# A decoder layer's first projection with GpSimd taken out: VectorE takes all modulation products, ScalarE takes h, TensorE takes the norm sum

## The chip, the cores and the metric

One NeuronCore of one Trainium2 chip runs the whole program. The time is device microseconds (us) of one execution. The engines are TensorE (PE in the profile, its weight loads PEld), VectorE (DVE), ScalarE (ACT), GpSimd (POOL) and SyncE (SP), which issues the DMAs. Each engine runs its own list of instructions in order; semaphores order them among each other.

## The reference

One decoder layer on 256 positions of 1024 channels. What matters here is its beginning:

```
mod = silu(c) @ w_ada + b_ada            # 6 x 1024 values: shift, scale, gate, twice
h   = rms_norm(x, norm1_g) * (1 + scale1) + shift1
proj = h @ w_in                          # q, k, v, z, xbc, dt
... attention on q, k, v; a state-space mixer on xbc, dt, z; output projection;
x = x + gate1 * mixed
x = x + gate2 * conv_ffn(rms_norm(x, norm2_g) * (1 + scale2) + shift2)
```

All arrays are float32.

## The kernel before

Activations lie transposed: channels on the 128 partitions, 256 positions along the free axis, so x is 8 tiles `xT[:, kt]`, and kt names a slice of 128 input channels. The first stage computes 16 blocks of 128 output channels (xbc, three blocks of z, and dt) in the 16 halves of the 8 PSUM banks, over the 8 slices, slice by slice, and in slice 0 also the part of v that comes from that slice.

For precision a product h·w is made from three float32r matmuls: whi·hhi, wlo·hhi and whi·hlo (`mm3`, L335). So each weight chunk is split after it lands: ScalarE rounds it into `whi` (L189) and VectorE subtracts to get `wlo` (L191). A slice has two chunks, of 1024 and of 912 columns. `P['subs']` says in how many pieces a chunk is loaded and split. A chunk in `PLAIN` is not split, but used as float32 in a single matmul, which PE runs in two passes. Here PE needs 8 x 16 = 128 products, that is 384 matmuls of 256 columns, for the 16 blocks.

h of a slice needs two sums over the 1024 inputs of c, the scale and the shift of those 128 channels (`mod`). Chunk 2·kt of `ada` gives the scale, chunk 2·kt+1 the shift. A chunk is multiplied with silu(c) (`cb`) and summed, either in one VectorE instruction (`ada_dve`, L239), or as a product on GpSimd (`ada_mul`, L244) that ScalarE then sums (`ada_sum`, L248). In the first stage chunks 0 and 1 and the odd ones go to VectorE, the 7 even ones from 2 on to GpSimd and ScalarE. `s1_next` lets GpSimd make `xr` = x times the norm's factor `rb` (L392). `s1_h` then makes the column `gcol` (L366), adds a bias (L253), and makes `hhi` on ScalarE (L380), `h` on VectorE (L384) and `hlo` on VectorE (L386).

The norm's factor for all positions comes first: squares `sq8`, added up into four tiles by VectorE, GpSimd and ScalarE, are summed over partitions by PE against ones (L267, in `rms_sum`), ScalarE takes the root (L270), VectorE the reciprocal (L272), and PE transposes it into PSUM (L291). PE runs 12 matmuls on ones ahead of that (L228) and 1 and 7 around the transposes (`keep_warm`, L296).

In this stage the order on every engine is the order of the code (`tc.manual_schedule`). SP issues its loads in the order of a list (`items`); a load of a weight chunk waits until the chunk 8 places earlier is split, and a load of `ada` until the chunk 9 places earlier is used. After the stage (from L450) the z projection (L785) and everything else follow, ordered by a scheduler within tables of units; the change leaves that code alone.

Of the kernel before, what the change touches and what calls it, by code (L numbers as in the profile page):

```python
# [11 lines left out]
AF = mybir.ActivationFunctionType  # L12
# [33 lines left out]

@with_exitstack
def mixer_ffn(ctx: ExitStack, tc: tile.TileContext, xT_d, c_d, vec_d, alog_d, ada_d,
# [272 lines left out]
    pool.memset(tri, 1.0)  # L321
    for o in (0, 256):
# [38 lines left out]
    first = list(range(12)) + [13, 12, 14, 15]  # L361
    final = (list(range(8)) + [12, 14, 15, 13, 8, 9, 10, 11], list(range(6)) + [14, 15, 12, 13, 8, 9, 10, 11, 6, 7],
             list(range(8)) + [14, 15, 12, 13, 8, 9, 10, 11], list(range(4)) + [14, 15, 12, 13, 8, 9, 10, 11, 4, 5, 6, 7])[P['final']]
    def s1_h(kt):
        g, shift = gcol[:, kt:kt + 1], mod[:, 2 * kt + 1:2 * kt + 2]
        dve.scalar_tensor_tensor(g, mod[:, 2 * kt:2 * kt + 1], sc1[:, kt:kt + 1], vec[:, V_N1 + kt:V_N1 + kt + 1],  # L366
                                 op0=OP.add, op1=OP.mult)
        ada_bias(2 * kt + 1, 2 * kt + 2)
        if kt == 0:
            xr = hbuf()  # L370
            if P["xr0"]:
                act.activation(rb, bank[7][:, 256:512], AF.Copy)
                pool.tensor_tensor(xr, xT[:, kt], rb, op=OP.mult)
            else:
                dve.tensor_tensor(xr, xT[:, kt], bank[7][:, 256:512], op=OP.mult)
        else:
            xr = X["xr"]
# [18 lines left out]
    def v0_mm(w):  # L396
        for j in range(2):
            c = slice(j * 512, j * 512 + 512)
            for t in range(2):
                o = bank[4 + 2 * j + t]  # L400
                pe.matmul(o, hhi[:, 0, blk(t)], w[0][:, c], start=True, stop=False)
                pe.matmul(o, hhi[:, 0, blk(t)], w[1][:, c], start=False, stop=False)
                pe.matmul(o, hlo[:, 0, blk(t)], w[0][:, c], start=False, stop=True)
        for j in range(2):
            c = slice(j * 512, j * 512 + 512)
            for t in range(2):
                o = bank[4 + 2 * j + t]
                if P["ev"][2 * j + t]:
                    dve.tensor_copy(vS[:, t, c], o)  # L409
                else:  # L410
                    act.activation(vS[:, t, c], o, AF.Copy)
# [8 lines left out]
    if P["scp"]:  # L420
        dve.tensor_scalar(sc1[:, 0:KT], vec[:, V_BADA:V_BADA + 16:2], 1.0, None, op0=OP.add)
    ada_dve(1)
    if not P["scp"]:
        dve.tensor_scalar(sc1[:, 0:KT], vec[:, V_BADA:V_BADA + 16:2], 1.0, None, op0=OP.add)
    for kt in range(KT):
        s1_h(kt)
        if kt < KT - 1:
            ada_mul(2 * kt + 2)
        if kt == 0:
            ws = [get(0)]  # L430
            w0 = get(0)
            ws.append(get(0))
        else:
            ws = [get(0), get(0)]
        if kt == 2:
            act.activation(warm, epsc, AF.Silu)
            dve.tensor_scalar(sc1[:, KT:], vec[:, V_BADA + 24:V_BADA + 32], 1.0, None, op0=OP.add)
            dve.scalar_tensor_tensor(gqk, vec[:, V_QG:V_QG + 1], SCALE, vec[:, V_KG:V_KG + 1], op0=OP.mult, op1=OP.mult)
        if kt < KT - 1:
            s1_next(kt + 1)  # L440
        if kt == 0:
            s1_mm(0, ws, first[:8])
            v0_mm(w0)
            s1_mm(0, ws, first[8:])
        else:
            s1_mm(kt, ws, final)
# [588 lines left out]
```

## Time and profile before

| | |
|---|---|
| median of 3 runs | 452.51 us (451.82 to 453.27) |
| profiled execution | 452.11 us, of which the span of instructions is 450.4 us |
| PE busy over the span | 433.8 us (96%) |
| DVE / ACT / POOL busy | 344.4 / 259.3 / 62.3 us |
| mean granted TensorE clock | 0.984 |

The span is from the first to the last instruction; what lies outside it is 1.7 us. The stage that the change touches takes the time up to the first z matmul (L785). Matmuls overlap, so PE's rows are longer than the distance from one to the next, and the distance is what one costs. The granted clock is 1.00 at 2.4 GHz and 0.50 at 1.2 GHz. The chip moved about 400 GB/s in the second to the fourth fortieth of the span, that is from 11 to 45 us.

### The profile page before, as it was taken

How to read it: one execution, taken by the hardware profiler on the slowest of the kernel's cores; microseconds unless marked ns; L12 is line 12 of the kernel's file. 1: busy time of each engine (PE TensorE's matmuls, PEld its weight loads, DVE VectorE, ACT ScalarE, POOL GpSimd, SP SyncE). 2: the span in 40 equal slices, each digit the busy share in tenths (PEclk: the TensorE clock that was granted, in tenths of full speed). 3: DMA queues.
4: the chain of work that ended last, by engine and by line, in shares of the span. 5: the costliest groups of instructions: out<-in, count | busy, mean ns of one | idle time of the engine just before them, and what ended most of it. 6: DMA issues, size and time to landing. Idle time of an engine off the chain costs nothing.

```text
span 450.4 us, 7730 instructions
## 1 busy us (share of the span) xinstructions
PE 433.8 (96%) x2900; PEld 384.7 (85%) x2900; DVE 344.4 (76%) x666; ACT 259.3 (58%) x523; POOL 62.3 (14%) x46
## 2 busy tenths in 40 slices
PE   7977999999999999999999989999999999999996
PEld 7876999867665566788899879999999999999996
DVE  4999992999567998647889478877777887777764
ACT  4535582945497668543237448566666665555540
POOL 3576400000000020100220000023322300000000
PEclk9789899999999999999999999999999999999999
DMA  7999674777558654245695073878677755654002
GB/s 287 399 402 400 203 239 149 255 283 268 175 175 283 229 207 182 94 141 188 222 412 206 20 307 110 282 246 258 228 254 260 234 185 186 193 174 156 0 1 95
DMA packets 31029, 96.71 MB, mean 215 GB/s; under 512 B 3712, under 2 KB 6672, under 8 KB 30992
## 3 DMA queue, kind: packets, MB, share of 16 engines
q1 hardware_dynamic: 30960, 96.20, 61.0%
q8 instruction: 23, 0.38, 0.4%
q14 instruction: 14, 0.11, 0.1%
q10 hardware_dynamic: 32, 0.02, 0.0%
HBM read 95.14 MB, written 1.06 MB: 214 GB/s over the span
## 4 chain that ended last, share of the span: by engine, by line
PE 73%; DMA 13%; DVE 7%; ACT 4%; SPq 1%; issue 1%; POOL 1%; DVEq 0%
PE bank L336 17%; PE bank L338 17%; PE bank L337 17%; PE bank L834 6%; DMA ada<-in_ada_dram 5%; PE bank L806 5%; PE bank L785 4%; DMA adax<-in_ada_dram 2%; DMA raw<-in_wv_dram 2%; DMA raw<-in_win_dram 2%; PE bank L906 1%; DVE wlo L191 1%; DMA xT<-in_xT_dram 1%; DVE ada L239 1%; DMA raw<-in_winq_dram 1%; DMA ab<-acd 1%
## 5 line engine op out<-in xcount | busy, mean ns | idle before, releaser
L191 DVE TENSOR_TENSOR wlo<-raw,whi 128x1024 fp32r<-128x1024 f32 (+3 forms) x112 | 137.4, 1235 | 15.4 <-ACT whi L189 15.0
L189 ACT ACTIVATE whi<-raw 128x1024 fp32r<-128x1024 f32 (+3 forms) x111 | 104.3, 953 | 36.7 <-PE bank L338 21.7
L336 PE MATMUL bank<-h2hi,whi 128*128 128x256 f32 x336 | 95.4, 285 | 2.1 <-ACT h2hi L876 1.9
L337 PE MATMUL bank<-h2hi,wlo 128*128 128x256 f32 x336 | 94.5, 283 | 0.0
L338 PE MATMUL bank<-h2lo,whi 128*128 128x256 f32 x336 | 93.9, 284 | 0.0
L336 PEld LDWEIGHTS bank<-h2hi,whi 128*128 128x128 f32 x336 | 64.4, 192 | 3.7 <-ACT h2hi L876 3.2
L244 POOL TENSOR_TENSOR ada<-ada,cb 128x1024 f32<-128x1024 f32 x13 | 33.4, 2569 | 241.8 <-DMA ada<-in_ada_dram 241.8
L337 PEld LDWEIGHTS bank<-h2hi,wlo 128*128 128x128 f32 x336 | 64.4, 192 | 0.0
L892 DVE SCALAR_TENSOR_TENSOR fbuf<-bank,vec,fbuf 128x255 f32<-128x255 f32 x84 | 40.4, 482 | 30.9 <-ACT fbuf L890 29.6
L338 PEld LDWEIGHTS bank<-h2lo,whi 128*128 128x128 f32 x336 | 63.8, 192 | 0.2 <-DVE h2lo L877 0.2
L336 PE MATMUL bank<-fsp,whi 128*128 128x256 f32 x176 | 49.8, 284 | 0.0
L337 PE MATMUL bank<-fsp,wlo 128*128 128x256 f32 x176 | 49.7, 283 | 0.0
L338 PE MATMUL bank<-fsp,whi 128*128 128x256 f32 x176 | 49.6, 283 | 0.0
L890 ACT ACTIVATE fbuf<-bank,vec 128x256 f32<-128x256 f32 x42 | 23.5, 561 | 36.4 <-PE bank L338 36.4
L806 PE MATMUL bank<-raw,h 128*128 128x512 f32 x96 | 44.3, 595 | 0.0
L336 PE MATMUL bank<-hhi,whi 128*128 128x256 f32 (+1 forms) x128 | 37.9, 296 | 3.7 <-DVE vS L409 2.4
L337 PE MATMUL bank<-hhi,wlo 128*128 128x256 f32 (+1 forms) x128 | 38.0, 297 | 2.2 <-DVE wlo L191 2.2
L338 PE MATMUL bank<-hlo,whi 128*128 128x256 f32 (+1 forms) x128 | 37.8, 295 | 0.7 <-DVE hlo L386 0.7
L336 PEld LDWEIGHTS bank<-fsp,whi 128*128 128x128 f32 x176 | 33.8, 192 | 0.1
L337 PEld LDWEIGHTS bank<-fsp,wlo 128*128 128x128 f32 x176 | 33.8, 192 | 0.0
L338 PEld LDWEIGHTS bank<-fsp,whi 128*128 128x128 f32 x176 | 33.7, 192 | 0.0
L239 DVE SCALAR_TENSOR_TENSOR ada<-ada,cb 128x1024 f32<-128x1024 f32 x25 | 30.3, 1216 | 3.5 <-DMA ada<-in_ada_dram 3.5
(222 smaller groups left out, 828.2 us busy)
## 6 DMA issues: line engine op xcount, KB each, us to landing
raw<-in_wup_dram SPq DMA_DIRECT2D x44, 512.0 KB, 4.2
ada<-in_ada_dram SPq DMA_DIRECT2D x38, 512.0 KB, 5.0
raw<-in_wdn_dram SPq DMA_DIRECT2D x22, 512.0 KB, 3.5
raw<-in_winq_dram SPq DMA_DIRECT2D x16, 512.0 KB, 4.3
raw<-in_wout_dram SPq DMA_DIRECT2D x16, 512.0 KB, 3.8
adax<-in_ada_dram SPq DMA_DIRECT2D x10, 512.0 KB, 7.6
raw<-in_win_dram SPq DMA_DIRECT2D x18, 256.0 KB, 7.0
raw<-in_winv_dram SPq DMA_DIRECT2D x6, 512.0 KB, 6.0
```

The lines of the kernel that those rows point to most:

```text
L189: act.activation(hi[:, c], t[:, c], AF.Copy)
L191: (pool if lo_on_pool(i) else dve).tensor_tensor(lo[:, c], t[:, c], hi[:, c].bitcast(F32), op=OP.subtract)
L239: dve.scalar_tensor_tensor(t, t, 1.0, sc, op0=OP.mult, op1=OP.mult, accum_out=mod[:, i:i + 1])
L244: pool.tensor_tensor(adas[i], adas[i], sc, op=OP.mult)
L336: pe.matmul(out, w[0], h[0], start=start, stop=False, skip_group_check=True)
L337: pe.matmul(out, w[1], h[0], start=False, stop=False, skip_group_check=True)
L338: pe.matmul(out, w[0], h[1], start=False, stop=stop, skip_group_check=True)
L785: pe.matmul(zo[i], w[:, blk(kt)], h32[:, kt, 0:S], start=(kt == 0), stop=(kt == KT - 1), skip_group_check=True)
L806: pe.matmul(bs[t], h32[:, kt, blk(t)], w[:, wc], start=(q4 == k2 == 0), stop=(kt == KT - 1))
L834: pe.matmul(sacc(d), w[:, blk(kt)], X["y32"][:, kt], start=(kt == d % 2 == 0), stop=(kt == 7), skip_group_check=True)
L890: act.activation(a, src, AF.Identity, bias=vec[:, V_FB + i:V_FB + i + 1], scale=vec[:, w + 2:w + 3])
L892: dve.scalar_tensor_tensor(a[:, s:], src[:, :S - s], vec[:, w + 2 - s:w + 3 - s], a[:, s:], op0=OP.mult, op1=OP.add)
```

## The change

- All 16 modulation products of the stage are `ada_dve` on VectorE; `ada_mul` and `ada_sum` are no longer called in it. `xr` is made by VectorE too. GpSimd has nothing to do in the stage after its masks.
- `h` is made by ScalarE from the same inputs as `hhi`.
- The 8 squares are 4 on ScalarE and 4 on VectorE, and PE sums all 8 (16 matmuls of one column in place of 8); GpSimd's square and VectorE's 4 adds are gone.
- 22 matmuls on ones in place of 12 ahead of the sums; 4 in place of 7 behind the transposes (`P['w1']`).
- The three terms run one after the other over the 8 blocks of a chunk: first whi·hhi for all, then wlo·hhi, then whi·hlo, except in the last slice, which keeps the old order. The second chunk of a slice is split behind the first chunk's matmuls in the code, and the next slice's products come behind that split.
- The v part of slice 0 (chunk 1, `-16` in `PLAIN`) is 4 float32 matmuls on `h` in place of 12 float32r ones, with no split. Its four copies out of PSUM are interleaved with the products.
- `P['subs']` is 1 for all slice chunks but the first: 10 chunks that were loaded and split in two pieces are now loaded and split in one. Chunk 1 (v) keeps its two loads.

```diff
-    for j in range(12):
+    for j in range(22):
         pe.matmul(bank[2][:, 0:128], ones, ones, start=True, stop=True)
...
-    pool.tensor_tensor(sq8[:, 3], xT[:, 3], xT[:, 3], op=OP.mult)
-    for kt in (5, 6, 7):
-        act.activation(sq8[:, kt], xT[:, kt], AF.Square)
-    for kt in (0, 1, 2, 4):
-        dve.tensor_tensor(sq8[:, kt], xT[:, kt], xT[:, kt], op=OP.mult)
-        if kt:
-            dve.tensor_tensor(sq8[:, 0], sq8[:, 0], sq8[:, kt], op=OP.add)
-    dve.tensor_tensor(sq8[:, 0], sq8[:, 0], sq8[:, 3], op=OP.add)
+    for kt in range(4, KT):
+        act.activation(sq8[:, kt], xT[:, kt], AF.Square)
+    for kt in range(4):
+        dve.tensor_tensor(sq8[:, kt], xT[:, kt], xT[:, kt], op=OP.mult)
+    def modulate1():
+        ada_dve(0)
+        dve.tensor_scalar(sc1[:, 0:KT], vec[:, V_BADA:V_BADA + 16:2], 1.0, None, op0=OP.add)
+        ada_dve(1)
+    r1 = rms_sum([sq8[:, kt] for kt in range(KT)], D, bank[7], modulate1)
...
+    def s1_gain(kt):
+        if kt:
+            ada_dve(2 * kt)
+            X["xr"] = hbuf()
+            dve.tensor_tensor(X["xr"], xT[:, kt], rb, op=OP.mult)
+            ada_dve(2 * kt + 1)
+        dve.scalar_tensor_tensor(gcol[:, kt:kt + 1], ...)
+        ada_bias(2 * kt + 1, 2 * kt + 2)
...
     def s1_h(kt):
...
         act.activation(hhi[:, kt], xr, AF.Identity, scale=g, bias=shift)
+        h = h32[:, kt, 0:S]
+        act.activation(h, xr, AF.Identity, scale=g, bias=shift)
-        dve.tensor_scalar(h, xr, g, shift, op0=OP.mult, op1=OP.add)
...
-    def s1_next(kt):
-        X["xr"] = hbuf()
-        pool.tensor_tensor(X["xr"], xT[:, kt], rb, op=OP.mult)
-        ada_sum(2 * kt)
-        ada_dve(2 * kt + 1)
...
     def v0_mm(w):
+        for j in range(2):
+            for t in range(2):
+                pe.matmul(bank[4 + 2 * j + t], h32[:, 0, blk(t)], w[:, j * 512:j * 512 + 512], start=True, stop=True)
...
+        if kt < KT - 1:
+            for k in range(3):
+                for i in which:
+                    one(i, k, k == 2)
+        else:
+            for i in which:
+                for k in range(3):
+                    one(i, k, k == 2)
```

On VectorE, one slice in the middle of the stage. Before (`ada` is a modulation chunk, `wlo` and `whi` a weight chunk's parts, `h` the slice's activations):

```order
L366 SCALAR_TENSOR_TENSOR gcol<-mod,sc_174,vec 128x1
L253 TENSOR_TENSOR mod<-mod,vec 128x1
L384 TENSOR_SCALAR h_161<-hbuf_156,gcol,mod 128x256
L191 TENSOR_TENSOR wlo_88<-raw_80,whi_83 128x512
L386 TENSOR_TENSOR hlo<-h_161,hhi 128x256
L191 TENSOR_TENSOR wlo_88<-raw_80,whi_83 128x512
L191 TENSOR_TENSOR wlo_89<-raw_73,whi_84 128x512
L191 TENSOR_TENSOR wlo_89<-raw_73,whi_84 128x400
L239 SCALAR_TENSOR_TENSOR ada_91,mod<-ada_91,cb 128x1024
```

The same place on VectorE with the change:

```order
L191 TENSOR_TENSOR wlo_87<-raw_80,whi_82 128x1024
L391 TENSOR_TENSOR hlo<-h_168,hhi 128x256
L191 TENSOR_TENSOR wlo_88<-raw_73,whi_83 128x912
L239 SCALAR_TENSOR_TENSOR adax_96,mod<-adax_96,cb 128x1024
L371 TENSOR_TENSOR hbuf_164<-xT,rb 128x256
L239 SCALAR_TENSOR_TENSOR ada_91,mod<-ada_91,cb 128x1024
L373 SCALAR_TENSOR_TENSOR gcol<-mod,sc_181,vec 128x1
L253 TENSOR_TENSOR mod<-mod,vec 128x1
```

A slice has two products and `xr` (`hbuf`) in place of one product and `h`, and its `wlo` are two instructions in place of up to four.

On ScalarE at the same place, with the change (before, `h` is not there, the products' sums L248 stand behind the splits, and `hhi` waits for GpSimd too):

```order
L189 ACTIVATE whi_82<-raw_80 128x1024 [waits DMAHW7_49,PE_49,Activation_49]
L385 ACTIVATE hhi<-hbuf_163,mod,gcol 128x256 [waits DVE_49]
L387 ACTIVATE h_168<-hbuf_163,mod,gcol 128x256
L189 ACTIVATE whi_83<-raw_73 128x912 [waits DMAHW2_49,PE_49,Activation_49]
L189 ACTIVATE whi_84<-raw_74 128x1024 [waits DMAHW1_49,DMAHW0_49,DMAHW3_49,PE_49,Activation_49]
```

The rounding of a slice's second chunk (912 columns) stands behind `hhi` and `h` of that slice.

On TensorE, the start of the program with the change:

```order
L228 MATMUL bank_67<-ones 128x128 x22
L267 MATMUL bank_72<-ones,sq_180 128x1 x16
L296 MATMUL bank_67<-ones 128x128
L291 MATMUL bank_72<-ident,rt_172 128x128 x2
L296 MATMUL bank_67<-ones 128x128 x4
L412 MATMUL bank_65<-hhi,whi_81 128x256 x2
L412 MATMUL bank_66<-hhi,whi_81 128x256 x2
```

Before, these rows are 12, 8, 1, 2 and 7 long, and the first blocks' three terms follow one another.

## Rows read from the trace of the kernel before

**Rows 1.** Engines by stretch: length, busy us (instructions), granted clock, DMA share, GB/s.

```profile
30.00:40.00 10.00, 8.93 (x69) 8.15 (x68) 9.89 (x11) 5.12 (x9) 7.13 (x5) 1.00 1.04 400
...
60.00:70.00 10.00, 10.00 (x86) 9.86 (x85) 8.29 (x19) 5.71 (x11) 0.00 (x0) 1.00 0.74 243
```

**Rows 2.** TensorE in time: start, us, operation: slice 1 and z begin.

```profile
28.65 0.41 PE L336 MATMUL bank<-hhi,whi 128*128 128x256 f32 x1
...
76.34 1.03 PE L785 MATMUL bank<-h,raw 128*128 128x256 f32 x4
```

**Rows 3.** VectorE in time, beside GpSimd and alone.

```profile
30.90 1.21 DVE L239 SCALAR_TENSOR_TENSOR adax<-adax,cb 128x1024 f32<-128x1024 f32 x1
...
32.05 2.33 DVE L366 SCALAR_TENSOR_TENSOR gcol<-mod,sc,vec 128x1 f32<-128x1 f32 x1
...
36.06 4.50 DVE L191 TENSOR_TENSOR wlo<-raw,whi 128x512 fp32r<-128x512 f32 x3
...
51.11 0.21 DVE L366 SCALAR_TENSOR_TENSOR gcol<-mod,sc,vec 128x1 f32<-128x1 f32 x1
51.24 0.15 DVE L253 TENSOR_TENSOR mod<-mod,vec 128x1 f32<-128x1 f32 x1
...
56.21 0.15 DVE L253 TENSOR_TENSOR mod<-mod,vec 128x1 f32<-128x1 f32 x1
...
57.73 1.78 DVE L191 TENSOR_TENSOR wlo<-raw,whi 128x512 fp32r<-128x512 f32 x3
...
60.70 0.15 DVE L253 TENSOR_TENSOR mod<-mod,vec 128x1 f32<-128x1 f32 x1
```

**Rows 4.** GpSimd in time: three of its seven products.

```profile
14.81 2.38 POOL L244 TENSOR_TENSOR ada<-ada,cb 128x1024 f32<-128x1024 f32 x1 [5.51 <-DMA ada<-in_ada_dram]
...
31.41 2.96 POOL L244 TENSOR_TENSOR adax<-adax,cb 128x1024 f32<-128x1024 f32 x1 [1.39 <-DMA adax<-in_ada_dram]
...
36.53 2.46 POOL L244 TENSOR_TENSOR ada<-ada,cb 128x1024 f32<-128x1024 f32 x1 [1.48 <-DMA ada<-in_ada_dram]
```

**Rows 5.** TensorE's warm-up and norm sums, two passes a matmul (several narrow stretches).

```profile
1.09 5.09 PE L228 MATMUL bank<-ones 128*128 128x128 f32 x24 [1.09 <-POOL ones L226]
...
5.52 0.66 PE L228 MATMUL bank<-ones 128*128 128x128 f32 x4
...
5.80 0.39 PE L228 MATMUL bank<-ones 128*128 128x128 f32 x2
...
8.37 0.36 PE L267 MATMUL bank<-ones,sq 128*128 128x1 f32 x2
...
8.48 0.36 PE L267 MATMUL bank<-ones,sq 128*128 128x1 f32 x2
...
10.44 0.35 PE L267 MATMUL bank<-ones,sq 128*128 128x1 f32 x1
...
10.65 0.35 PE L267 MATMUL bank<-ones,sq 128*128 128x1 f32 x1
```

**Rows 6.** VectorE and ScalarE: steps of the start and of a slice.

```profile
11.55 0.17 DVE L272 RECIPROCAL rt<-rt 128x2 f32<-128x2 f32 x1 [0.26 <-ACT rt L270]
...
13.03 0.42 DVE L375 TENSOR_TENSOR hbuf<-xT,bank 128x256 f32<-128x256 f32 x1
...
13.99 0.36 ACT L382 ACTIVATE rb<-bank 128x256 f32<-128x256 f32 x1
...
25.85 0.96 ACT L189 ACTIVATE whi<-raw 128x912 fp32r<-128x912 f32 x1
...
51.48 0.60 ACT L380 ACTIVATE hhi<-hbuf,mod,gcol 128x256 fp32r<-128x256 f32 x1 [3.58 <-DVE mod L253]
```

**Rows 7.** The chain that ended last: float32 matmuls of 512 columns, two passes each.

```profile
106.06 3.43 PE bank L806 x8
```

**Rows 8.** All of TensorE's waits from 76 us to the end.

```profile
PE bank L336 <- ACT h2hi L876: 1.9, 5, 0.4
PE bank L648 <- ACT qk L642: 0.7, 1, 0.7
```

More of the change, by code (lines that the diff above doesn't have):

```diff
@@ L24 @@
 LAG = 2
-PLAIN = [0, 1, 2, 3, 4, 5, 6, 8, 10, 12, 14, 16, 18, 20, 22, 24, 26, 28, 29, 30, 31, 32, 33, 34, 35, 36, 45, 46]
+PLAIN = [-16, 0, 1, 2, 3, 4, 5, 6, 8, 10, 12, 14, 16, 18, 20, 22, 24, 26, 28, 29, 30, 31, 32, 33, 34, 35, 36, 45, 46]
 NEG = -1.0e30
@@ L328, in mixer_ffn @@
                        pattern=[[-1, 128]], channel_multiplier=1)
-    r1 = rms_sum([sq8[:, kt] for kt in (5, 6, 7, 0)], D, bank[7], lambda: ada_dve(0))
+    for kt in range(4, KT):
[7 more added lines that the diff above has]
+    r1 = rms_sum([sq8[:, kt] for kt in range(KT)], D, bank[7], modulate1)
     keep_warm(P["w0"], bank[2][:, 0:128])
@@ L363, in mixer_ffn @@
              list(range(8)) + [14, 15, 12, 13, 8, 9, 10, 11], list(range(4)) + [14, 15, 12, 13, 8, 9, 10, 11, 4, 5, 6, 7])[P['final']]
-    def s1_h(kt):
[L365 to L377, printed above, removed]
+    def s1_gain(kt):
[4 more added lines that the diff above has]
+            ada_dve(2 * kt + 1)
+        dve.scalar_tensor_tensor(gcol[:, kt:kt + 1], mod[:, 2 * kt:2 * kt + 1], sc1[:, kt:kt + 1],
+                                 vec[:, V_N1 + kt:V_N1 + kt + 1], op0=OP.add, op1=OP.mult)
+        ada_bias(2 * kt + 1, 2 * kt + 2)
+        if not kt:
+            X["xr"] = hbuf()
+            dve.tensor_tensor(X["xr"], xT[:, 0], bank[7][:, 256:512], op=OP.mult)
+    def s1_h(kt):
+        g, shift, xr = gcol[:, kt:kt + 1], mod[:, 2 * kt + 1:2 * kt + 2], X["xr"]
         w = split_steps()
@@ L380, in s1_h @@
         act.activation(hhi[:, kt], xr, AF.Identity, scale=g, bias=shift)
-        if kt == 0 and not P["xr0"]:
+        h = h32[:, kt, 0:S]
+        act.activation(h, xr, AF.Identity, scale=g, bias=shift)
+        if kt == 0:
             act.activation(rb, bank[7][:, 256:512], AF.Copy)
-        h = h32[:, kt, 0:S]
-        dve.tensor_scalar(h, xr, g, shift, op0=OP.mult, op1=OP.add)
         next(w)
@@ L388, in s1_h @@
             pass
-    def s1_next(kt):
-        X["xr"] = hbuf()
-        pool.tensor_tensor(X["xr"], xT[:, kt], rb, op=OP.mult)
-        ada_sum(2 * kt)
-        ada_dve(2 * kt + 1)
     def v0_mm(w):
         for j in range(2):
-            c = slice(j * 512, j * 512 + 512)
             for t in range(2):
[L400 to L411, printed above, removed]
+                pe.matmul(bank[4 + 2 * j + t], h32[:, 0, blk(t)], w[:, j * 512:j * 512 + 512], start=True, stop=True)
@@ L413, in s1_mm, with v0_evac, one @@
+    def v0_evac(j, t):
+        o, c = bank[4 + 2 * j + t], slice(j * 512, j * 512 + 512)
+        if t:
+            act.activation(vS[:, t, c], o, AF.Copy)
+        else:
+            dve.tensor_copy(vS[:, t, c], o)
     def s1_mm(kt, ws, which):
-        for i in which:
+        def one(i, k, last):
             c, o = divmod(off[i], 1024)
             m = 16 if i == 12 else 128
-            mm3(s1_acc(i)[:m], sl(ws[c], slice(o, o + m)), (hhi[:, kt], hlo[:, kt]),
-                start=(kt == 0 and i in (0, 2, 4, 6, 8, 10, 13, 14)), stop=(kt == KT - 1))
@@ L420, in mixer_ffn @@
[L420 to L424, printed above, removed]
-    for kt in range(KT):
-        s1_h(kt)
+            w, h = sl(ws[c], slice(o, o + m)), (hhi[:, kt], hlo[:, kt])
+            pe.matmul(s1_acc(i)[:m], w[k % 2], h[k // 2], start=(kt == k == 0 and i in (0, 2, 4, 6, 8, 10, 13, 14)),
+                      stop=last and kt == KT - 1, skip_group_check=True)
@@ new lines, in s1_mm @@
+        if kt < KT - 1:
+            for k in range(3):
+                for i in which:
+                    one(i, k, k == 2)
+        else:
+            for i in which:
+                for k in range(3):
+                    one(i, k, k == 2)
+    for kt in range(KT):
+        if kt == 0:
+            s1_gain(0)
+            s1_h(0)
+            ws = [get(0)]
+            s1_mm(0, ws, first[:8])
+            ada_dve(2)
+            w0 = get(0)
+            v0_mm(w0)
+            done(1)
+            ws.append(get(0))
+            X["xr"] = hbuf()
+            dve.tensor_tensor(X["xr"], xT[:, 1], rb, op=OP.mult)
+            v0_evac(0, 0)
+            v0_evac(0, 1)
+            ada_dve(3)
+            v0_evac(1, 0)
+            v0_evac(1, 1)
+            s1_mm(0, ws, first[8:])
+            dve.scalar_tensor_tensor(gcol[:, 1:2], mod[:, 2:3], sc1[:, 1:2], vec[:, V_N1 + 1:V_N1 + 2],
+                                     op0=OP.add, op1=OP.mult)
+            ada_bias(3, 4)
+        else:
+            s1_mm(kt, [ws[0]], final[:8])
+            ws.append(get(0))
+            if kt == 2:
+                act.activation(warm, epsc, AF.Silu)
+                dve.tensor_scalar(sc1[:, KT:], vec[:, V_BADA + 24:V_BADA + 32], 1.0, None, op0=OP.add)
+                dve.scalar_tensor_tensor(gqk, vec[:, V_QG:V_QG + 1], SCALE, vec[:, V_KG:V_KG + 1], op0=OP.mult,
+                                         op1=OP.mult)
+            if kt < KT - 1:
+                s1_gain(kt + 1)
+            s1_mm(kt, ws, final[8:])
@@ L427, in mixer_ffn @@
         if kt < KT - 1:
-            ada_mul(2 * kt + 2)
-        if kt == 0:
+            s1_h(kt + 1)
             ws = [get(0)]
[L431 to L446, printed above, removed]
     zs = T([128, 8, S], "zs", tag="big_z")
```

2 lines of the change are left out of this document (1 added, 1 removed).

## The prediction, made before the changed kernel ran

> **What bounds the kernel now.** I read the busy shares by stretch first, then TensorE in time, then VectorE and GpSimd beside it, and last TensorE's waits of the rest. The stretch from 30 to 40 us shows the first stage: VectorE is busy for 9.89 of 10 us, GpSimd for 7.13, the DMAs carry all they can, and TensorE has holes [rows 1]. From 60 to 70 us GpSimd is idle and TensorE runs without holes: 86 matmuls in 10 us, 0.12 us each (a few records may be missing). So a slice of 48 matmuls needs 48 x 0.12 = 5.76 us of TensorE. Slice 1 begins at 28.65 us and the z matmuls at 76.34 [rows 2]: 47.7 us for seven slices that need 7 x 5.76 = 40.3, and 28.65 us before the first of them. After 76 us TensorE waits for 2.6 us in all [rows 8], so what the stage ends earlier should come through to the end.
>
> The holes come from VectorE, and VectorE is slow there because of GpSimd. The same three `wlo` pieces take 4.50 us from 36.06 on and 1.78 from 57.73 on; `gcol`, one value per partition, takes 2.33 us from 32.05 on and 0.21 from 51.11 on [rows 3]. GpSimd's product from 31.41 on ends at 34.37, where `gcol` ends too (34.38), and its product from 36.53 on lies inside the slow pieces [rows 4]. That the loads do this instead is spoken against by the product at 30.90: between two GpSimd products, in the stretch with the DMAs full, it takes 1.21 us.
>
> The Trainium skill ("SBUF — State Buffer", section "Who interferes with whom") says that VectorE and GpSimd share a port pair as an exclusive lock: whoever comes second waits for the other's whole instruction, also a VectorE instruction with two SBUF inputs. The trace agrees with 2.33 against 0.21 us. By it the whole stretch goes when GpSimd falls silent; if the two only shared a rate, `gcol` could not have grown by 2.1 us.
>
> **The change, part by part: the start.** The 24 warm-up passes take 5.09 us, 0.21 each, which is the 1.2 GHz level; the last come closer: four from 5.52 on, two of these from 5.80 on [rows 5]. So the clock rises near 5.6 us. 44 passes are then 21 at 0.21 and 23 at 0.11, until 8.1 us. The sums are 16 matmuls, 32 passes of 0.11 (8.37 to 8.48), 3.5 us, until 11.6. Root and reciprocal follow by about 12.2, where the reciprocal now ends at 11.72 [rows 6]. The transposes are four passes, some 0.8 us, and `xr` can begin at 13.0, where it begins now (13.03): it was held by product 1, which now comes sooner since four adds of about 0.42 us are gone from VectorE ahead of it. So the dropped adds pay for the longer warm-up and sums, and this part is worth 0. If the sums run at the lower clock, 0.21 a pass (10.44 to 10.65), it costs up to 5.6 us (a rival below); if they are ready sooner, it can give back 1 us.
>
> **From there to slice 1.** `hhi` is ready at 14.1 (0.42 and 0.60 us). ScalarE then makes `h` (0.6), `rb` (0.36) and the second half of the first `whi` (about 0.6, an estimate by columns from the 0.96 us of 912), VectorE its `wlo` (0.6, a third of the 1.78 for three pieces): 16.2. TensorE by then has 12 matmuls of the first 24 left, until 17.6. The v part is 8 float32 passes at 3.43 us [rows 7], until 21.1 (the 12 float32r matmuls that go cost 12 x 0.23 = 2.8 by the columns, so this swap alone costs 0.6, but it takes a split of 1024 columns, 1.2 us, from VectorE). The second 24 matmuls, 2.9 us, bring 24.0. Slice 1 begins then if its `hhi` is there: VectorE's list after 16.2 is product 2 (1.15, from 30.90 to the next at 32.05; its data landed at 14.81 [rows 4]), a `wlo` (1.1), `xr` (0.4), two copies of 512 columns (about 0.6 each, as a `wlo` piece of that size), product 3 (1.15) and the columns (0.3), to 21.5; ScalarE's `whi` and `hhi` behind it make 23.0. So slice 1 starts at 24.0 in place of 28.65: 4.6 us gained.
>
> **The slices.** VectorE alone, without GpSimd, goes from bias to bias in 60.70 - 56.21 = 4.49 us [rows 3]. It now gets a product, +1.15, `xr` for `h`, about 0, and one piece per chunk, about -0.05: 5.6 us, under TensorE's 5.76. But ScalarE has `h` now, and the rounding of a slice's second chunk stands behind it. From the bias on: 0.24 to `hhi` (51.24 to 51.48), 1.1 for `hhi` and `h`, 0.96 for the rounding: 2.3 us. VectorE has bias, `wlo` of 1024 columns (1.2) and `hlo` (0.42) to do meanwhile, 1.8 us, and so waits 0.5 us for the 912 columns. A step is then 6.1 us, a bit longer than TensorE's. Bounds: 5.76 where the wait is hidden by TensorE's lead, and 6.5 where a handover of 0.1 us is paid at each of four crossings between the engines. I take 6.05.
>
> Slice 1's bias stands near 21.4; slice 2's at 28.5, a step and 1 us more, since ScalarE copies v in front of it. Five steps further, slice 7's bias is at 58.8, its `hlo` 1.75 later at 60.5. The last slice keeps the old order and needs `hlo` for its third matmul: 46 x 0.12 = 5.5 more, end at 66.0. TensorE by itself would be at 24.0 + 7 x 5.76 = 64.3. The z matmuls begin 76.34 - 66.0 = 10.3 us earlier.
>
> **Edits at nothing.** Term by term order: hides the wait for `wlo` and `hlo` behind 8 matmuls (1 us) each; without it every step would show these waits of up to 1 us. Loads in one piece: the same bytes in the same order on SP's queue; a chunk is whole later by up to half of its 1.3 us at 400 GB/s, and VectorE gets to it later than the loads do from slice 2 on. Three matmuls on ones fewer: 6 passes, TensorE would have waited for `hhi` there. ScalarE's table load in slice 2 (it stands there now too) lies in its wait for the bias, 3.6 us long in the row at 51.48 [rows 6].
>
> **Sum.** The profiled execution took 452.11 us, span 450.4; the median of the runs shown is 452.51, 0.4 more. 452.11 - 10.3 = 441.8 us.
>
> **Rivals.** First, TensorE is the bound: its lead from the start covers VectorE's longer steps in all slices. The end is at 64.3, 12.0 us gained, 440.1 us. For it speaks that 5.6 us of VectorE work is less than 5.76; against it the wait for ScalarE.
>
> Second, the start comes late. If the clock does not rise during the warm-up, 44 passes end at 10.5, the sums 6.8 us later at 17.3, `xr` at 18.6, 5.6 us behind; everything follows, and the gain is 4.7 us: 447.4. Against it: the rise near 5.6 us, with the same matmuls up to there. In between lies a clock that falls while the one-column sums run (now it stands at the lower level at 10.44, after a pause between warm-up and sums): 1 to 2.5 us, 443 to 444. The Trainium skill ("TensorE: Matmul & The Clock Gate", section "What's actually happening") has the throttled state as the default, to which an idle engine returns; the fall after the pause agrees. Whether one-column passes hold the clock no run shows.
>
> Third, part of the gain is given back after 66 us: VectorE's convolutions or the loads for q come no sooner, and TensorE waits where it does not now. At half, 447 us. Against it: TensorE's 2.6 us of waits in 374 us, and the loads at 243 GB/s from 60 on [rows 1], far from full.
>
> Fourth, and slower: the stretched VectorE instructions are the loads' doing, not GpSimd's. The DMAs stay full until the stage's chunks are in, VectorE keeps its stretch (2.7 us on three pieces, 2.1 on `gcol`, so about 4.8 a slice) and has 1.15 us more to do: steps of 10.9 us for four or five slices, then 6.1. The last bias comes near 77 us and the end near 84, 8 us later than now: 460 us. It decides from a step of (76.34 - 5.5 - 1.75 - 28.5) / 5 = 8.1 us on. The product at 30.90 speaks against it.
>
> **Chances.** The forecast 0.54, its own range 440.5 to 443.5 from steps of 5.8 to 6.3 us. TensorE as the bound 0.25, late start 0.08, given back 0.09, slower 0.04. The range from 438.5 to 446.0 takes in the first two, 1.5 us of an earlier start below them, and the lighter forms of the next two. A change under 0.3% (1.4 us) could not be told from none; it would need a mixture of losses, 0.02. Faster 0.94, same 0.02, slower 0.04.
>
> **What would show it.** Right: `gcol` at 0.2 us in all slices; bias to bias near 6 us with VectorE's gap before the 912-column `wlo`, ended by ScalarE; slice 1 on TensorE near 24 us, z near 66; TensorE at the full clock from about 17 us on. The start is wrong if `xr` begins more than 1 us away from 13.0 or the sums run at 0.21 a pass. The main step is wrong if VectorE's instructions of the stage are still stretched, or if a step is over 6.5 us for another reason; the last if TensorE's waits after the stage grow beyond 2.6 us.

## The result and the profile after

The changed kernel took 441.75 us (median of 4 runs, 440.92 to 442.02), beside 452.31 us (median of 4) for the kernel before on the same chip: a ratio of 0.9756 with a 95% interval of 0.9725 to 0.9788. Of the executions told of below one is left out of the ratios and medians, the profiled one of the first run with GpSimd's reads, which took 537.33 us at a mean granted clock of 0.749 where the others had 0.98 or more. The span of the profiled execution fell from 450.4 to 439.2 us, by 11.2.

Of this, 10.37 us are gained up to the first z matmul, which moves from 76.34 [rows 2] to 65.97. They fall into two parts. Slice 1 begins at 24.08 in place of 28.65, 4.57 us; the seven slices from there to z take 41.89 us in place of 47.69, 5.80 us. The missing 0.8 us come behind the stage and are told of at the end of the part on the prediction.

The busy times of the changed kernel, from the first part of its page (share of the span, number of instructions), show where the work went: GpSimd's is nearly halved, the others' hardly moves.

```profile
PE 431.4 (98%) x2926; PEld 382.5 (87%) x2926; DVE 332.1 (76%) x663; ACT 253.8 (58%) x506; POOL 34.1 (8%) x31
```

VectorE has 7 products and 7 `xr` more to do (and 8 `h`, 4 adds and the split of v's 1024 columns less) and is still busy for 12.3 us less than before (344.4). That is only possible if many of its instructions got shorter. The engines from 30 to 40 us, in the columns of [rows 1]:

```profile
30.00:40.00 10.00, 10.00 (x84) 9.84 (x84) 9.11 (x18) 6.13 (x8) 0.00 (x0) 1.00 1.03 409
```

From 30 to 40 us VectorE now does 18 instructions where it did 11, in less busy time, with the DMAs as full as before (409 GB/s against 400). TensorE has no hole there.

VectorE in time, one step of the changed kernel, from one bias (L253) to the next:

```profile
46.53 0.22 DVE L373 SCALAR_TENSOR_TENSOR gcol<-mod,sc,vec 128x1 f32<-128x1 f32 x1
46.66 0.16 DVE L253 TENSOR_TENSOR mod<-mod,vec 128x1 f32<-128x1 f32 x1
46.73 1.23 DVE L191 TENSOR_TENSOR wlo<-raw,whi 128x1024 fp32r<-128x1024 f32 x1
47.98 0.42 DVE L391 TENSOR_TENSOR hlo<-h,hhi 128x256 fp32r<-128x256 f32 x1
48.84 1.11 DVE L191 TENSOR_TENSOR wlo<-raw,whi 128x912 fp32r<-128x912 f32 x1 [0.43 <-ACT whi L189]
49.86 1.22 DVE L239 SCALAR_TENSOR_TENSOR adax<-adax,cb 128x1024 f32<-128x1024 f32 x1
...
52.62 0.15 DVE L253 TENSOR_TENSOR mod<-mod,vec 128x1 f32<-128x1 f32 x1
```

The step is 52.62 - 46.66 = 5.96 us. `gcol` takes 0.22 us, as in the row at 51.11 in [rows 3] and not as in the one at 32.05, and the pieces of `wlo` have their short durations. The only gap stands before the 912 columns, 0.43 us, ended by ScalarE. All waits of VectorE from 25 to 66 us (total, times, longest) are that one:

```profile
DVE wlo L191 <- ACT whi L189: 3.1, 7, 0.6
```

TensorE in time, from the warm-up to slice 1, and z:

```profile
1.09 6.76 PE L228 MATMUL bank<-ones 128*128 128x128 f32 x44 [1.09 <-POOL ones L226]
7.69 3.63 PE L267 MATMUL bank<-ones,sq 128*128 128x1 f32 x32
...
13.98 1.81 PE L412 MATMUL bank<-hhi,whi 128*128 128x256 f32 x8
...
17.54 3.59 PE L398 MATMUL bank<-raw,h 128*128 128x512 f32 x8
...
24.08 1.12 PE L412 MATMUL bank<-hhi,whi 128*128 128x256 f32 x8
...
53.46 1.22 PE L412 MATMUL bank<-hhi,whi 128*128 128x256 f32 x8
...
59.41 0.38 PE L412 MATMUL bank<-hhi,whi 128*128 128x256 f32 x1
...
60.37 0.38 PE L412 MATMUL bank<-hlo,whi 128*128 128x256 f32 x1
...
65.97 2.33 PE L798 MATMUL bank<-h,raw 128*128 128x256 f32 x10
```

Slices 1 and 2 take 5.75 and 5.77 us, the 48 matmuls of 0.12 us that TensorE needs. From slice 3 on (35.60) they begin 5.95 us apart, as the last two do here (53.46 and 59.41): TensorE then goes at VectorE's step and loses 0.2 us a slice. In the last slice the third matmul, the first on `hlo`, begins at 60.37, 0.96 us behind the first one, where two matmuls without a wait take 0.24. The view of TensorE's waits lists none of this, since its rows overlap; the distances between the starts show it.

The steps of the start on VectorE, which answer to the first two of [rows 6]: the reciprocal is 0.1 us later than there, `xr` 0.4 us earlier.

```profile
11.65 0.17 DVE L272 RECIPROCAL rt<-rt 128x2 f32<-128x2 f32 x1
...
12.66 0.42 DVE L378 TENSOR_TENSOR hbuf<-xT,bank 128x256 f32<-128x256 f32 x1 [0.66 <-PE bank L291]
```

TensorE's waits from 66 us to the end are 2.8 us, 0.2 more than in [rows 8]:

```profile
PE bank L338 <- ACT h2hi L889: 1.9, 5, 0.4
PE bank L661 <- ACT qk L655: 0.9, 1, 0.9
```

### The profile page after: what moved, and what is told of

It is laid out like the page before. It is cut to its first block, busy times and chain, and to the rows that moved or that the text cites. A ratio compares the mean times of both kernels' runs of the same rounds, so it can differ in the third digit from the quotient of the medians.

```text
span 439.2 us, 7681 instructions
## 1 busy us (share of the span) xinstructions
PE 431.4 (98%) x2926; PEld 382.5 (87%) x2926; DVE 332.1 (76%) x663; ACT 253.8 (58%) x506; POOL 34.1 (8%) x31
## 4 chain that ended last, share of the span: by engine, by line
PE 74%; DVE 9%; DMA 8%; ACT 6%; issue 1%; POOL 1%; SPq 0%; ACTq 0%; POOLq 0%
PE bank L338 15%; PE bank L339 15%; PE bank L340 15%; PE bank L847 6%; PE bank L819 6%; PE bank L798 4%; DMA ada<-in_ada_dram 3%; DVE adax L239 2%; DMA raw<-in_win_dram 2%; DVE wlo L191 2%; ACT whi L189 2%; DVE ada L239 2%; DMA raw<-in_winv_dram 1%; PE bank L822 1%; PE bank L823 1%; DMA xT<-in_xT_dram 1%
## 5 line engine op out<-in xcount | busy, mean ns | idle before, releaser
L191 DVE TENSOR_TENSOR wlo<-raw,whi 128x1024 fp32r<-128x1024 f32 (+2 forms) x100 | 124.6, 1246 | 20.8 <-ACT whi L189 20.4
L189 ACT ACTIVATE whi<-raw 128x1024 fp32r<-128x1024 f32 (+2 forms) x99 | 101.9, 1035 | 39.6 <-PE bank L340 25.5
L905 DVE SCALAR_TENSOR_TENSOR fbuf<-bank,vec,fbuf 128x255 f32<-128x255 f32 x84 | 40.3, 481 | 29.8 <-ACT fbuf L903 28.5
L244 POOL TENSOR_TENSOR ada<-ada,cb 128x1024 f32<-128x1024 f32 x11 | 28.3, 2577 | 273.2 <-DMA ada<-in_ada_dram 273.2
L239 DVE SCALAR_TENSOR_TENSOR ada<-ada,cb 128x1024 f32<-128x1024 f32 x27 | 32.7, 1218 | 3.7 <-DMA ada<-in_ada_dram 2.4
L819 PEld LDWEIGHTS bank<-raw,h 128*128 128x128 f32 x96 | 17.3, 190 | 15.3 <-issue 14.9
L847 PE MATMUL bank<-y,raw 128*128 128x256 f32 x128 | 28.7, 380 | 0.0
L847 PEld LDWEIGHTS bank<-y,raw 128*128 128x128 f32 x128 | 23.9, 190 | 3.0
```

Source lines behind the costliest of these rows:

```text
L189: act.activation(hi[:, c], t[:, c], AF.Copy)
L191: (pool if lo_on_pool(i) else dve).tensor_tensor(lo[:, c], t[:, c], hi[:, c].bitcast(F32), op=OP.subtract)
L819: pe.matmul(bs[t], h32[:, kt, blk(t)], w[:, wc], start=(q4 == k2 == 0), stop=(kt == KT - 1))
L847: pe.matmul(sacc(d), w[:, blk(kt)], X["y32"][:, kt], start=(kt == d % 2 == 0), stop=(kt == 7), skip_group_check=True)
L905: dve.scalar_tensor_tensor(a[:, s:], src[:, :S - s], vec[:, w + 2 - s:w + 3 - s], a[:, s:], op0=OP.mult, op1=OP.add)
```

## The experiments

The theory was that GpSimd's products held up VectorE, and that VectorE then held up TensorE. The main rival was that the full DMAs stretched VectorE. The other parts of the change came as claims of their own: the new order of the terms and the longer warm-up were each costed as needed, and `h` on ScalarE as the cause of the wait of 0.4 us.

**GpSimd's work put back, with no use made of it.** To the changed kernel two GpSimd products per slice (0 to 6) are added, of 1024 and 256 columns. They start behind `h` of the slice, and nothing needs their results.

```
+        pool.tensor_copy(nz[:, 0, 0:1], h32[:, kt, 0:1])
+        pool.tensor_tensor(nz[:, 0], nz[:, 1], nz[:, 1], op=OP.mult)
+        pool.tensor_tensor(nz[:, 0, 0:256], nz[:, 1, 0:256], nz[:, 1, 0:256], op=OP.mult)
```

> The changed kernel, with useless GpSimd work put back: in each of slices 0 to 6, once h of the slice is there, a tensor_tensor of 128x1024 and one of 128x256 on a tile that nobody else uses. No other engine waits for it. Theory (GpSimd's reads hold VectorE up): VectorE's instructions beside it stretch as before (gcol over 2 us, wlo pieces doubled), the step from bias to bias grows from 5.95 us by about 2.5 to 4 us, the z matmuls begin 15 to 25 us later than 66 us, and the time is 457 to 467 us, slower than the kernel before. Rival (the gain came from the order of the terms, the loads in one piece and the shorter lists, and the stretch from the loads): GpSimd's idle work costs nothing, 441 to 443 us.

Measured: 454.81 us, a ratio to the kernel before of 1.0058 (1.004 to 1.0076): GpSimd work that nobody needs takes back the whole gain and a little more. The slowdown was expected, but larger: 457 us or more. The same kernel was then profiled once more.

> The same kernel as in the first run with GpSimd reads, for its profile at the full TensorE clock. Theory: steps from bias to bias of about 7.8 us, the 912-column wlo at 2.4 to 2.6 us beside GpSimd and 1.1 without, z near 79 us (66 + 6 x 1.9 + some 2 in slice 0), 454 to 456 us. Rival (the loss lies elsewhere than on VectorE): z near 66 us all the same.

Its one time was 456.53 us, 0.5 above the expected range. VectorE in that run, from one bias to the next:

```profile
40.28 0.15 DVE L253 TENSOR_TENSOR mod<-mod,vec 128x1 f32<-128x1 f32 x1
...
42.45 2.55 DVE L191 TENSOR_TENSOR wlo<-raw,whi 128x912 fp32r<-128x912 f32 x1 [0.43 <-ACT whi L189]
44.92 1.63 DVE L239 SCALAR_TENSOR_TENSOR adax<-adax,cb 128x1024 f32<-128x1024 f32 x1
...
48.09 0.15 DVE L253 TENSOR_TENSOR mod<-mod,vec 128x1 f32<-128x1 f32 x1
```

and GpSimd there:

```profile
42.14 1.89 POOL L355 TENSOR_TENSOR nz<-nz 128x1024 f32<-128x1024 f32 x1
44.11 1.36 POOL L356 TENSOR_TENSOR nz<-nz 128x256 f32<-128x256 f32 x1
```

The step is 7.81 us. Exactly the two VectorE instructions that meet GpSimd are longer: the 912 columns by 2.55 - 1.11 = 1.44 us, the product by 1.63 - 1.22 = 0.41. Together that is 1.85 us, which is what the step grew by (7.81 - 5.96). The rows also show how: GpSimd's first product ends at 44.03, and 44.03 plus the 1.11 us that the 912 columns take alone is 45.1, near where they end (45.00). So they waited until that GpSimd instruction was over; had VectorE gone on at half its rate, the 912 columns would have ended before 44.7. GpSimd's second product seems to have waited in its turn: it takes 1.36 us for a quarter of the columns. `gcol` keeps its 0.21 us, against what was expected of it, since GpSimd has finished before it. The z matmuls begin at 78.94, 13.0 us later than in the changed kernel: the 79 expected of this run, and less than the 81 to 91 expected of the first. My first price for GpSimd's work was too high: a GpSimd product of 1024 columns lasts 1.89 us here, and I had taken 2.4 to 3.0 from [rows 4].

**GpSimd busy, but only writing.** In place of the two products, three fills of 1024 columns.

```
-        pool.tensor_tensor(nz[:, 0], nz[:, 1], nz[:, 1], op=OP.mult)
-        pool.tensor_tensor(nz[:, 0, 0:256], nz[:, 1, 0:256], nz[:, 1, 0:256], op=OP.mult)
+        for _ in range(3):
+            pool.memset(nz[:, 0], 1.0)
```

> As the run with reads, but the GpSimd work of each slice is three memsets of 128x1024, which write and read nothing. If any GpSimd work on the memory holds VectorE up, the step grows as there, by the memsets' length, and the time is 455 to 465 us. If only its reads do, as the Trainium skill's SBUF page (section Who interferes with whom) has it for VectorE instructions with two inputs, VectorE's instructions keep their lengths and the time stays at 441 to 443 us.

Measured: 441.93 us, ratio 0.9772 (0.9743 to 0.9802), the same as the changed kernel. GpSimd and, beside it, VectorE in that run:

```profile
43.17 2.98 POOL L356 MEMSET nz<- 128x1024 f32 x3
```

```profile
43.49 1.11 DVE L191 TENSOR_TENSOR wlo<-raw,whi 128x912 fp32r<-128x912 f32 x1 [0.43 <-ACT whi L189]
44.52 1.22 DVE L239 SCALAR_TENSOR_TENSOR ada<-ada,cb 128x1024 f32<-128x1024 f32 x1
```

Nearly 3 us of GpSimd work lie beside two VectorE instructions, and both keep their durations. It is GpSimd's reads that matter, not that it is busy. The Trainium skill ("SBUF — State Buffer", section "Who interferes with whom") says both: a VectorE instruction with two SBUF inputs contends with a GpSimd instruction that reads SBUF, and not with one that only writes it. The two runs agree, with 1.11 us beside the fills and 2.55 beside the product.

**The products alone.** In the kernel before, only the 7 even products and `xr` go to VectorE; all else stays.

```
-        pool.tensor_tensor(X["xr"], xT[:, kt], rb, op=OP.mult)
-        ada_sum(2 * kt)
+        dve.tensor_tensor(X["xr"], xT[:, kt], rb, op=OP.mult)
+        ada_dve(2 * kt)
...
-        if kt < KT - 1:
-            ada_mul(2 * kt + 2)
```

> The kernel before with one part of the change alone: the 7 even products and xr of the first stage go from GpSimd and ScalarE to VectorE; order of terms, loads, h on VectorE, warm-up and sums stay. Theory: nearly the whole gain, since VectorE's step is 4.49 + 1.15 + 0.4 = 6.0 us without GpSimd and slice 1 starts near 25 us instead of 28.65; z at 66 to 68 us, time 442 to 445 us. Rival (the order of the terms and the one-piece loads make the gain): at most 3 us, 449 to 453 us.

Measured: 440.73 us, ratio 0.9751 (0.9715 to 0.9787), faster than the 442 to 445 expected. This edit alone has the whole gain. It also takes seven sums (`ada_sum`) off ScalarE, but those are off in the run with GpSimd's reads too, where the gain is gone. TensorE in that run begins slice 1 at 24.21 and z at 65.16 (66 to 68 expected), both with the old start and the old order of terms (the first matmuls behind v, of slice 1 and of z):

```profile
21.27 0.36 PE L336 MATMUL bank<-hhi,whi 128*128 128x256 f32 x1
...
24.21 0.28 PE L336 MATMUL bank<-hhi,whi 128*128 128x256 f32 x1
...
65.16 5.35 PE L783 MATMUL bank<-h,raw 128*128 128x256 f32 x24
```

VectorE's step there, bias to bias, is 57.96 - 52.06 = 5.90 us.

To compare this kernel with the whole change side by side, both were run once more.

> The changed kernel once more, as the measure for the two beside it: 441.75 us, within 0.6.

> The kernel before with the products and xr on VectorE and nothing else, beside the changed kernel. If the rest of the change is worth nothing, the two are equal within 0.5 us; if the rest is worth its 1 us of term order or its 0.5 us a slice of wait, this one is slower by 1 us or more (442.8 or more against 441.75).

Measured: 441.71 us (0.977, 0.9756 to 0.9783) for the whole change and 441.11 us (0.9764, 0.9746 to 0.9781) for the products alone. The intervals lie on each other. What else the change does sums to nothing that these runs can tell; single parts of it may cancel each other.

**`h` back on VectorE**, in the changed kernel:

```
-        act.activation(h, xr, AF.Identity, scale=g, bias=shift)
+        dve.tensor_scalar(h, xr, g, shift, op0=OP.mult, op1=OP.add)
```

> The changed kernel with h of every slice back on VectorE. Theory of the step: VectorE does 5.5 us of work and waits 0.43 us for ScalarE's rounding of the 912 columns, which stands behind h; with h on VectorE (0.33 us) that wait goes, so a step is 5.85 in place of 5.95 us, and the time stays within 1 us of 441.75 (440.5 to 442.3). Rival (moving h off VectorE is worth its 0.33 us a slice): 7 x 0.33 = 2.3 us slower, 444 us.

Measured: 441.0 us, ratio 0.9752 (0.9722 to 0.9782), no different from the changed kernel. VectorE in that run:

```profile
40.61 0.15 DVE L253 TENSOR_TENSOR mod<-mod,vec 128x1 f32<-128x1 f32 x1
...
42.26 0.42 DVE L391 TENSOR_TENSOR hlo<-h,hhi 128x256 fp32r<-128x256 f32 x1
42.59 1.10 DVE L191 TENSOR_TENSOR wlo<-raw,whi 128x912 fp32r<-128x912 f32 x1
...
46.37 0.15 DVE L253 TENSOR_TENSOR mod<-mod,vec 128x1 f32<-128x1 f32 x1
```

The gap before the 912 columns is gone, and the step is 5.76 us: 0.2 shorter, although `h` is one instruction more on VectorE. So ScalarE's `h`, with the rounding behind it, did cause the wait, as predicted, and moving `h` there gained nothing.

**The old order of the terms**, in all slices of the changed kernel (`if kt < KT - 1:` becomes `if False:` in `s1_mm`):

> The changed kernel with the three terms of each block one after the other in all slices, as in the kernel before. Theory (VectorE's step of 5.95 us sets the pace, and the last slice has the old order anyway): each slice begins up to 1 us later behind hlo and makes it up before the next, so z stays at 66 us and the time at 441.75, within 0.7 us. Rival (the order of the terms hides waits that were on the path): 0.5 to 1 us a slice, 3 to 6 us slower, 445 to 448 us.

Measured: 442.15 us, ratio 0.9777 (0.9755 to 0.9799); z begins at 66.14 against 65.97, and VectorE's step is 5.95 us. TensorE in that run, in slice 7:

```profile
60.31 0.27 PE L412 MATMUL bank<-hhi,wlo 128*128 128x256 f32 x1
60.55 0.39 PE L412 MATMUL bank<-hlo,whi 128*128 128x256 f32 x1
```

The matmul on `hlo` comes 0.24 us behind the one ahead of it, in place of 0.12. In slices 4 to 7 TensorE loses 0.2 us here, at the third matmul and the one behind it, where with the new order slices 4 to 6 lose it just ahead of and behind their first. So the order moves the wait and does not remove it: VectorE's step of 5.95 us sets the pace either way. The order of the terms is worth nothing that can be told.

**The short warm-up**, in the changed kernel (`range(22)` becomes `range(12)`):

> The changed kernel with 12 in place of 22 warm-up matmuls. Theory of the start: TensorE pauses from 6.2 us until the first squares, the clock falls near 9 us as in the kernel before, some 20 of the 32 passes of the sums run at 0.21 us in place of 0.11, the reciprocal and xr come about 2 us later, and since VectorE's list runs without slack from there the time grows by 1.5 to 2 us, to 443.5. Rival (the longer warm-up does nothing that counts): the same 441.75 us within 0.5.

Measured: 443.06 us, ratio 0.9789 (0.9772 to 0.9806). That is 1.3 us above the changed kernel, near the 1.5 to 2 expected, but the intervals overlap, and what the trace shows is not what I expected. TensorE in that run:

```profile
1.09 5.49 PE L228 MATMUL bank<-ones 128*128 128x128 f32 x24 [1.09 <-POOL ones L226]
6.83 3.94 PE L267 MATMUL bank<-ones,sq 128*128 128x1 f32 x32 [0.26 <-DVE sq L325]
...
25.19 1.00 PE L412 MATMUL bank<-hhi,whi 128*128 128x256 f32 x7
```

The sums do not run slowly: 32 passes from 6.83 to 10.63, 0.12 each, the first 3 us of them at a granted clock of 1.00. In the kernel before there was a pause of 2.06 us ahead of them, ended by ScalarE, since the first tile that it sums is a square of ScalarE:

```profile
8.24 2.98 PE L267 MATMUL bank<-ones,sq 128*128 128x1 f32 x16 [2.06 <-ACT sq L314]
```

Here the first tile is VectorE's, and the pause is 0.26 us. Nor is `xr` later: it starts at 12.69 against 12.66, because VectorE's reciprocal stands behind product 1 in VectorE's list, here right behind its end at 11.68:

```profile
11.68 0.16 DVE L272 RECIPROCAL rt<-rt 128x2 f32<-128x2 f32 x1
...
12.69 0.42 DVE L378 TENSOR_TENSOR hbuf<-xT,bank 128x256 f32<-128x256 f32 x1 [0.66 <-PE bank L291]
```

What is later is slice 0, and the granted clock says why. It is the column before the last two; the run with the short warm-up:

```profile
15.00:17.00 2.00, 2.00 (x10) 1.93 (x10) 1.95 (x4) 0.98 (x2) 0.00 (x0) 0.50 1.02 415
17.00:18.00 1.00, 1.00 (x8) 1.00 (x8) 1.00 (x2) 0.00 (x0) 0.00 (x0) 0.73 1.05 426
```

and the changed kernel:

```profile
15.00:17.00 2.00, 1.97 (x17) 1.95 (x17) 1.96 (x4) 0.97 (x1) 0.00 (x0) 1.00 1.04 419
```

Both fall to the 1.2 GHz level behind the sums. The changed kernel is back at 2.4 GHz from 15 us on, this one only within 17 to 18, so that from 15 to 17 us it does 10 matmuls against 17, and slice 1 starts at 25.19 against 24.08. In all nine profiles of this study with 22 matmuls ahead of the sums the clock is back at the upper level 3 to 4 us after it fell, in this one after more than 6. What that costs these runs do not show: with the long warm-up too slice 1 begins anywhere from 24.08 to 25.02, and the intervals of the times overlap.

**Rounding ahead.** In the changed kernel ScalarE rounds the 912 columns of the next slice before it makes `hhi` and `h`, from slice 2 on.

```
     def round_early(i):
+        early[i] = hi_r()
+        rounded.add(i)
+        act.activation(early[i][:, :n], raws[i][:, :n], AF.Copy)
...
+        if kt >= 2:
+            round_early(st["split"] + 1)
```

> The changed kernel with one move: from slice 2 on ScalarE rounds the slice's second chunk (912 columns) ahead of hhi and h, in the 3 us in which it waits for the bias. VectorE's wait of 0.43 us a slice goes, its step falls from 5.95 to 5.5 us, and TensorE's 5.75 becomes the pace; z at 64.3 to 65, time 440.0 to 440.9 us, 1 to 1.7 less than the changed kernel. Rival (TensorE's lead already covers the longer step, and only the last slice's wait counts): no more than 0.5 us.

Measured: 440.75 us, ratio 0.974 (0.9727 to 0.9754). The gap on VectorE is gone, a step is 51.20 to 56.64, 5.44 us, and slice 1 to z takes 40.30 us against 41.89. Not all of that reaches the end in the profiled execution, where the warm-up took 7.58 us and slice 1 began at 25.02.

**The same, with both ends of the stage smoothed.** In addition, the last two blocks of slice 0 follow the other six, and the first chunk of the last slice runs term by term.

```
-            s1_mm(0, ws, first[8:])
+            s1_mm(0, ws, first[8:14])
+            s1_mm(0, ws, first[14:])
...
-        if kt < KT - 1:
+        if kt < KT - 1 or which[0] == 0:
```

> As the run with the rounding ahead, with two more moves on TensorE: in slice 0 the last two blocks, whose bank is copied last, get their terms behind the other six, and in the last slice the first chunk's blocks run term by term too. By the theory slice 1 begins at 23.8 in place of 24.1 us and nothing waits in the last slice: z near 64, time 439.7 to 440.6 us.

Measured: 440.75 us, ratio 0.9745 (0.9723 to 0.9768), with slice 1 at 24.17 (23.8 expected) and z at 64.67. The time is that of the run before it, so the two ends are worth nothing that can be told. This version was run again beside the changed kernel.

> The changed kernel with the rounding ahead and the two moves on TensorE, beside the changed kernel. Theory: slice 1 to z takes 40.3 to 40.5 us in place of 41.9, so 1 to 1.5 us faster than the changed kernel where the starts agree. Rival: no difference, the 1 us seen is the start's own scatter.

Measured: 440.1 us, ratio 0.9729 (0.9716 to 0.9743), clear of the changed kernel's interval beside it (0.9756 to 0.9783): 1.6 us faster, and the best version of this study. TensorE in that run, slice 1 and z:

```profile
24.18 1.12 PE L424 MATMUL bank<-hhi,whi 128*128 128x256 f32 x8
...
64.49 5.35 PE L811 MATMUL bank<-h,raw 128*128 128x256 f32 x24
```

VectorE's step is 5.43 us (51.05 to 56.48), as with the rounding ahead alone. Seven slices in 40.31 us are 5.76 us each, 48 matmuls at 0.12 without a gap: here TensorE is the bound.

## Why the prediction was right, step by step

- **What bounds the kernel.** Right, and shown. GpSimd's reads put back alone cost 13 us and stretch just the instructions beside them; its writes cost nothing. The slower rival, that the loads stretch VectorE, falls: at 409 GB/s VectorE's instructions are short.
- **The start.** The time was right: `xr` at 12.66 (13.0 predicted), the v part at 17.54 (17.6), slice 1 at 24.08 (24.0). The reason given was right in part. Product 1 comes sooner since the adds are gone, and ends with the root just ahead of the reciprocal (11.60 and 11.62). That the v part came on time is in part luck: the sum has TensorE held until 16.2 by the second `wlo` of slice 0, which was ready at 15.72. TensorE was late by itself: its 24 matmuls ahead of v took 3.56 us (13.98 to 17.54) in place of 2.88, since the first of them ran at 1.2 GHz and the fifth waited for the second half of `whi`, ready at 15.0. And the kernel with the products alone keeps the adds, the old sums and the short warm-up, and starts slice 1 at 24.21. So the gain of the start comes from GpSimd's silence between 13 and 24 us; the rework of the norm is worth about 0, as the prediction has it. Where the kernel before lost that time the prediction does not say, and its trace does. TensorE stood for 2.42 us until VectorE had copied v (VectorE's product ahead of the copy took 3.40 us beside one of GpSimd's, 1.22 alone), and behind that pause the clock fell to the lower level (a mean of 0.55 from 26 to 27 us). The last 24 matmuls of slice 0 took 4.06 us there (24.59 to 28.65); with the products alone there is no such pause, the clock stays at 1.00 and they take 2.94 (21.27 to 24.21). So the stretched VectorE cost TensorE twice, by the wait and by the clock behind it. The kernel before, TensorE and then the engines in the columns of [rows 1]:

```profile
24.59 0.36 PE L336 MATMUL bank<-hhi,whi 128*128 128x256 f32 x1 [2.42 <-DVE vS L409]
```

```profile
26.00:27.00 1.00, 1.00 (x8) 0.86 (x7) 1.00 (x2) 1.00 (x2) 0.66 (x1) 0.55 1.02 398
```

- **The warm-up.** The prediction pays for the longer warm-up and gives no reason for it; ahead of the run with the short one I held that it keeps the sums at full speed. They keep it without. What is longer without it is the stretch at 1.2 GHz behind the sums, in the one profile there is, at a loss that these runs can't tell from the scatter of the start.
- **A step of the slices.** Right: 5.96 us (6.05 predicted), with a wait of 0.43 us for ScalarE before the 912 columns (0.5). The wait is paid on TensorE only from slice 3 on, since its lead covers the first two slices. Slice 7's `hlo` is ready at 60.3 (60.5 predicted): TensorE's first use of it starts at 60.37. And z begins at 65.97 (66.0). That TensorE by itself would need 40.3 us, the first rival's number, is shown by the version that rounds ahead.
- **Term order at nothing.** Without the new order I had seen waits of up to 1 us a step. The run with the old order has z 0.17 us later in all. The price was wrong by its size and by its kind: TensorE loses 0.2 us a slice with either order, because VectorE's step is 0.2 us longer than TensorE's, and the order only sets at which matmul.
- **Nothing given back.** Right, but for 0.2 us; TensorE's waits behind the stage are 2.8 us against 2.6. The span gained 0.8 us more than the sum. The last result tile on VectorE came at 446.52 us before and comes at 435.78 now, 10.74 us earlier, so about 0.4 us of this lie between z and that tile and 0.4 in what follows it, the store and the end. No experiment was made on either, and what they are stays open. The profiled execution took 440.92 us, so the sum was 0.9 us too long against its own kind of number; that the median of the runs, 441.75, lies on it is chance.

## What to carry to other kernels

Where VectorE and GpSimd work at the same time and VectorE sets the pace, compare one VectorE instruction of the same shape beside GpSimd and alone. If it grows by about as long as GpSimd's instruction still runs, GpSimd's help can cost more than it gives, and giving its reading work to VectorE can shorten VectorE's own time, as here by 12.3 us. When a change has many parts, run the one part that the profile blames by itself: here moving the products and `xr` alone had the whole gain. After such a change look at what each engine's next wait is, and read it from the distances between starts where the rows overlap; here it was one instruction in the wrong place on ScalarE, worth 1.6 us between slice 1 and z.

## What the hardware showed that was not expected

- GpSimd's fills (0.95 to 1 us for 1024 columns) cost VectorE nothing, while a product cost it nearly all the time that the product still had to run: 1.44 us of the 1.58 from 42.45 to 44.03. I had expected a difference, not that it would be so complete.
- The stretch reaches instructions of a few elements. In the run with GpSimd's products a VectorE instruction on 8 columns took 0.57 us, started while GpSimd's product of 256 columns was running (36.16 to 37.52), and ended with it. In the changed kernel the same instruction takes 0.17 us.

```profile
36.97 0.57 DVE L460 TENSOR_SCALAR sc<-vec 128x8 f32<-128x8 f32 x1
```

- The same warm-up does not always take the same time. The 44 passes took from 6.76 to 7.92 us in nine executions of kernels that begin with the same passes, and slice 1 began at 24.08 with 6.76 us and at 25.02 with 7.58. This scatter alone is as large as what most of the parts of this change were expected to be worth.
- With all eight squares summed by TensorE the clock fell behind the one-column sums, not while they ran: it was 1.00 up to 11 us in the changed kernel and up to 10 us with the short warm-up, whose sums end 0.6 us earlier, and then fell to 0.50. In the kernel before, with its pause of 2.06 us ahead of them, it fell while they ran: the mean is 0.52 from 9 to 10 us. The prediction had this case as a rival in which the sums themselves are slow. The changed kernel:

```profile
10.00:11.00 1.00, 1.00 (x11) 1.00 (x11) 1.00 (x4) 0.00 (x0) 0.00 (x0) 1.00 1.03 365
11.00:12.00 1.00, 0.92 (x6) 0.66 (x7) 0.95 (x5) 0.64 (x2) 0.00 (x0) 0.64 0.96 340
```
